# A hybrid mLSTM and SSD decoder layer on one core: a state computed at the end, and five re-timed places

## The chip, the cores and the metric

The kernel runs on 1 core of one Trainium2 chip. The metric is device time in microseconds (us) of one execution. Engines are named as in the profile: PE (matmul) with PEld (its weight loads), DVE (vector), ACT (scalar), POOL (GpSimd) and SP, which here only issues DMAs. The engines run side by side, each takes its own instructions in order, and semaphores make one wait for another.

## The reference, cut to what matters

One layer of a decoder trunk for a prompt of 256 tokens (zero state) and a batch of 8 x 8 sample tokens (given state), 320 tokens in all, 2048 wide, all in float32.

```
u = x @ w_in                                  # 2048 -> q, k, v, o, gates, z, xbc, dt
h_m, C, n, m = mlstm_mixer(q, k, v, o, ...)   # 4 heads, 256 x 256 state each
h_s, S, ...  = ssd_mixer(z, xbc, dt, ...)     # 16 heads
x = layer_norm(ALPHA * x + concat(h_m, h_s) @ w_out, ln1_g, ln1_b)
f = (silu(g) * val) @ w_down                  # g, val = conv3(x @ w_up), width 5504 each
x = layer_norm(ALPHA * x + f, ln2_g, ln2_b)
# mLSTM state at a chunk's end:
C_new = decay * C + einsum('bsh,bshd,bshe->bhde', w_end, k, v)
n_new = decay * n + einsum('bsh,bshd->bhd', w_end, k)
```

Results are the two outputs (`y_prompt`, `y_sample`) and twelve states. `p_C` and `p_n`, the prompt's last mLSTM state, are among them; nothing else in the layer reads them. Since the prompt starts at zero, the kernel forms them at one stroke from all 256 tokens: per head, C = (w k)^T [v, 1], with the column of ones giving n.

## The kernel before, in words

Activations lie transposed: 128 features on the partitions, 320 tokens along the free axis. Each weight tile of 512 KB (`raw`) is fetched by SP, split by ACT into `hi` and by DVE into `lo` (lines 74 and 75, four 128 x 128 blocks at a time), and each block takes three fast matmuls of 320 columns at line 232: hi times the activation's high half, hi times its low half, lo times its high half. The halves are `XH`, `XL` (input), `MH`, `ML` (mixer's output) and `HH`, `HL` (FFN). `run_groups` walks over the output units, 16 k-tiles each, in steps of 4 k-tiles (12 matmuls). Splits are made four steps ahead, from at most four `raw` tiles.

Everything else is a background task, a generator in `Tasks`. While the program is written out, `tasks.clk` adds up a nominal time of the matmuls; a task that yields n goes on when the clock has moved n further (a bare `yield` is 2500), and `pump` lets tasks run after each step. So a pause in a task sets only where its instructions stand in the engines' order, between which weight matmuls. `ensure` and `drain` go on without matmuls between. On chip nothing is paused; an instruction waits for its data or its turn.

The stages, in order:

1. Start. `ones` is set and 9 matmuls on it run (the name is `warm`). `x_load` fetches the prompt in four column pieces, `xs_load` the sample as two halves of its columns (k-tiles 0 to 7 on partitions 0 to 63, 8 to 15 on 64 to 127). `x_transpose` turns each k-tile (two matmuls with the identity for the prompt; one for the sample, which for k below 8 gives k and k + 8). ACT and DVE split it into `XH`, `XL`.
2. Gates. `keep_x` adds XH and XL on POOL, multiplies with the gate weights `gw` (8 + 16 columns of w_in, fetched by SP as many short runs at lines 466 and 467), in four portions c, and stores x to DRAM (`xT`). The SSD tasks wait for the gates.
3. Mixer, beside the matmuls of w_in. SSD tasks, then for each of 4 mLSTM heads: `ml_scores`, `ml_chunks` (the sample's states, in sets n0 = 0, 2, ..., 14), `ml_out` (the head's output and its group norm, with `rsqrt` as three rounds on DVE), `o_task`, `mix_parts`. `ml_prompt_state` transposes k, scales it (`kt`), multiplies it with `VT` (v by tokens, with the column of ones), copies the result out and stores `p_C`.
4. w_out, whose first four units need the four parts of the mixer's output in turn (`ensure(("mix", s))`); first norm; the FFN in three portions (w_up, then w_down each).
5. End. `down_task` of the last portion transposes each of 16 tiles back and takes statistics (line 1571). After the last tile: aggregate all 16 (line 1644), inverse root by ACT and five DVE steps (1645 to 1652), rows of mean and bias by three matmuls on the identity (`nbr`), twelve matmuls that spread them, eight DVE steps for the prompt (line 1676), and for the sample ACT twice (1671, 1673) and POOL once (1674) per 512 columns.

Of the kernel before, what the change touches and what calls it, by code (L numbers as in the profile page):

```python
# [170 lines left out]
def _hybrid_step(ctx, tc, I, O):  # L171
# [11 lines left out]
    def f32(ap):  # L183
        return ap.bitcast(F32)
# [215 lines left out]
    def x_transpose(c, kks=range(4)):  # L400
        t = box["x", c]
        if kks[-1] == 3:
            flags.add(("xt", c))
            del box["x", c]
        for kk in kks:
            k = 4 * c + kk
            ps = bank()
            for i in range(2):
                transpose(ps[:, 128 * i:128 * i + 128], t[:, i, 128 * kk:128 * kk + 128])
            parts = [(k, 0, 256)]  # L410
            if k < 8:
                transpose(ps[:, 256:384], xs_in[:, 128 * k:128 * k + 128])
                parts = [(k, 0, NT), (k + 8, NT, 384)]
            parts = [(kx, slice(256 if a else 0, 256 if b == 256 else NT), ps[:, a:b]) for kx, a, b in parts]
            for kx, o, src in parts:
                A.activation(XH(kx)[:, o], src, AF.Copy)
            for kx, o, src in parts:
                V.tensor_tensor(XL(kx)[:, o], src, f32(XH(kx))[:, o], ALU.subtract)  # L418
# [22 lines left out]
    xs_src = I["x_sample"].rearrange("b t f -> (b t) f")  # L441

    def xs_load(eng, a, b):
        for e in range(2):
            eng.dma_start(xs_in[64 * e:64 * e + 64, a:b], xs_src[:, 1024 * e + a:1024 * e + b])
# [640 lines left out]
    def ml_prompt_state():  # L1086
        yield from wait("setup")
        pn = sm([128, 8])
        for h in range(4):
            yield from wait(("k", 2 * h + 1))  # L1090
            K = box["K"]
            ps = bank()
            for i in range(2):
                for e in range(2):
                    c = 256 * i + 128 * e
                    transpose(ps[:, c:c + 128], K[:, 2 * h + e, 128 * i:128 * i + 128])
            kt = mt("T2", [128, 2, 256])
            for i in range(2):
                A.activation(kt[:, i, :], ps[:, 256 * i:256 * i + 256], AF.Copy, scale=TT2[:, i, h:h + 1])
            yield  # L1100
            yield from wait(("v", 2 * h + 1))
            yield
            cn = mt("T2", [128, 2, 256])
            for e in range(2):
                ps = bank()
                for i in range(2):
                    mm(ps[:, 0:258], kt[:, i, 128 * e:128 * e + 128], box["VT"][:, i, h, :], i == 0, i == 1)
                A.activation(cn[:, e, :], ps[:, 0:256], AF.Copy)
                V.tensor_copy(pn[:, 2 * h + e:2 * h + e + 1], ps[:, 256:257])
                yield  # L1110
            dma(O["p_C"][0, 0, h].rearrange("(e p) f -> p e f", p=128), cn)
        ps = bank()
        transpose(ps[0:8, 0:128], pn)
        po = sm([8, 128])
        V.tensor_copy(po, ps[0:8, 0:128])
        yield
        gdma(O["p_n"][0, 0].rearrange("h (e p) -> (h e) p", p=128), po)
# [48 lines left out]
    def ml_chunks():  # L1166
# [27 lines left out]
        for h in range(4):  # L1194
# [7 lines left out]
            for x in range(2):  # L1202
# [27 lines left out]
                yield 5000  # L1230
            flags.add(("acc", h))

    def ml_out(h):
# [32 lines left out]
        rs = yield from rsqrt(mp, var, GN_EPS, [128, 3], 1500)  # L1266
# [7 lines left out]
        yield 8000  # L1274
# [261 lines left out]
    lnst = fsm([128, 3, 16, 6])  # L1536
# [16 lines left out]
    def down_task(j, m, ps):  # L1553
# [16 lines left out]
        for i in range(3):  # L1570
            V.bn_stats(lnst[:, i, m, :], pt[:, 128 * i:128 * i + 128])
        if m == 14:
            A.activation(fin["sd"], fin["eps"], AF.Sqrt)
# [6 lines left out]
    def times_g(m, pt):  # L1580
# [4 lines left out]
        V.tensor_tensor(r2[:, c], pt[64:128, 256:384], gbc[64:128, c], ALU.mult)  # L1585

    def gb_rows():
# [22 lines left out]
    for j in range(3):  # L1610
# [13 lines left out]
        if j == 2:  # L1624
# [15 lines left out]
    mv, var, nb2, rs, u = fsm([128, 3, 2]), fsm([128, 3]), fsm([128, 3]), fsm([128, 3]), fsm([128, 3])  # L1640
    nbc, nbr = fsm([128, 3, 5], F32R), fr("dg", [5, 384], F32R)
    G.memset(f32(nbc), 1.0)
    for i in range(3):
        V.bn_aggr(mv[:, i, :], lnst[:, i, :, :])
    A.activation(fin["sd"], mv[:, :, 1], AF.Sqrt, bias=fin["eps"][:, 0:1])
    V.tensor_scalar(var, mv[:, :, 1], LN_EPS, None, ALU.add)
    V.reciprocal(rs, fin["sd"])
    V.tensor_tensor(u, rs, rs, ALU.mult)
    V.tensor_tensor(u, u, var, ALU.mult)
    V.tensor_scalar(var, u, 0.375, -1.25, ALU.mult, ALU.add)  # L1650
    V.tensor_tensor(u, u, var, ALU.mult)
    V.scalar_tensor_tensor(rs, u, 1.875, rs, ALU.add, ALU.mult)
    V.scalar_tensor_tensor(nb2, mv[:, :, 0], -1.0, rs, ALU.mult, ALU.mult)
    V.tensor_copy(nbc[:, :, 0:2], bcl(nb2, 2))
    V.tensor_tensor(nbc[:, :, 2], nb2, f32(nbc[:, :, 0]), ALU.subtract)
    ps = bank()
    for i in range(3):
        transpose(ps[0:5, 128 * i:128 * i + 128], f32(nbc[:, i, :]))
    for i in range(3):
        t = slice(128 * i, 128 * i + 128)  # L1660
        V.tensor_copy(nbr[:, t], ps[0:5, t])
    times_g(15, fin["pt"])
    ys = O["y_sample"].rearrange("b t f -> (b t) f")
    for c in range(4):
        s = slice(512 * c, 512 * c + 512)
        for i in range(3):
# [3 lines left out]
            if i == 2:  # L1670
                A.activation(t, t, AF.Copy, scale=rs[64:128, i:i + 1])
                w2 = fr("rx", [128, 512])[64:128]
                A.activation(w2, w[64:128, :], AF.Copy)
                G.tensor_tensor(t, t, w2, ALU.add)  # L1674
            else:
                V.scalar_tensor_tensor(t, t, rs[:, i:i + 1], w, ALU.mult, ALU.add)
# [4 lines left out]
    dma(*late)
# [64 lines left out]
```

## Time and profile before

| | us |
|---|---|
| median of 3 runs | 1546.82 |
| lowest, highest | 1544.77, 1548.61 |
| the profiled execution | 1550.87 |
| its span, first to last instruction | 1549.0 |
| PE busy within it | 1521.4 |
| DVE, ACT, POOL busy | 980.7, 773.4, 306.1 |

PE is busy nearly all the time, so what counts is where it isn't, where its granted clock is low, and how much it is given to do. A page of the profile has the whole; the other views cut it by stretches of time, by waiting engine, or row by row. A row of the timeline gives the start, the length, the engine and line, then output <- inputs; a float32 matmul stands there as two instructions, a fast one (`fp32r` operands) as one. Rows of PE overlap, since a matmul is listed up to its end in the pipeline: the distance from start to start is what one costs.

### The profile page before, as it was taken

How to read it: one execution, taken by the hardware profiler on the slowest of the kernel's cores; microseconds unless marked ns; L12 is line 12 of the kernel's file. 1: busy time of each engine (PE TensorE's matmuls, PEld its weight loads, DVE VectorE, ACT ScalarE, POOL GpSimd, SP SyncE). 2: the span in 40 equal slices, each digit the busy share in tenths (PEclk: the TensorE clock that was granted, in tenths of full speed). 3: DMA queues.
4: the chain of work that ended last, by engine and by line, in shares of the span. 5: the costliest groups of instructions: out<-in, count | busy, mean ns of one | idle time of the engine just before them, and what ended most of it. 6: DMA issues, size and time to landing. Idle time of an engine off the chain costs nothing.

```text
span 1549.0 us, 28113 instructions
## 1 busy us (share of the span) xinstructions
PE 1521.4 (98%) x10518; PEld 1488.8 (96%) x10518; DVE 980.7 (63%) x1959; ACT 773.4 (50%) x1540; POOL 306.1 (20%) x651
## 2 busy tenths in 40 slices
PE   8999999999999999999999999999999999999996
PEld 7999999998999999999999999999999999999995
DVE  4676557666687587687777445566544555656765
ACT  3655434444545454566665345555433555555332
POOL 5213331134411142233330000000000000002201
PEclk8999999999999999999999999999999999999997
DMA  9556677577665554455544454554454555455542
GB/s 252 161 150 163 183 208 225 160 211 226 209 204 174 193 180 138 126 165 149 150 150 140 154 147 146 163 150 138 149 157 146 148 151 163 141 149 170 159 145 77
DMA packets 268900, 254.39 MB, mean 164 GB/s; under 512 B 18513, under 2 KB 263265, under 8 KB 268636
## 3 DMA queue, kind: packets, MB, share of 16 engines
q1 hardware_dynamic: 263612, 248.49, 53.8%
q0 software_dynamic: 4848, 3.91, 1.0%
q8 instruction: 82, 1.34, 0.4%
q14 instruction: 54, 0.44, 0.1%
q10 hardware_dynamic: 304, 0.20, 0.0%
HBM read 231.56 MB, written 20.43 MB: 163 GB/s over the span
## 4 chain that ended last, share of the span: by engine, by line
PE 93%; DVE 2%; DMA 2%; POOL 1%; ACT 1%; issue 1%; SPq 1%; POOLq 0%; DVEq 0%; ACTq 0%
PE bk L232 90%; PE bk L238 2%; DMA T<-w_in 1%; DVE lo L75 1%; DMA rx<-xT 0%; SPq L61 0%; ACT hi L74 0%; POOL big L1674 0%; SPq L466 0%; ACT MH L1320 0%; POOL T L193 0%; POOL T L968 0%; POOL T L811 0%; DVE HL L1531 0%; POOL T L981 0%
## 5 line engine op out<-in xcount | busy, mean ns | idle before, releaser
L75 DVE TENSOR_TENSOR lo<-raw,hi 128x512 fp32r<-128x512 f32 (+2 forms) x800 | 558.0, 708 | 393.5 <-ACT hi L74 390.6
L74 ACT ACTIVATE hi<-raw 128x512 fp32r<-128x512 f32 (+2 forms) x800 | 486.3, 616 | 454.3 <-PE bk L232 429.5
L232 PE MATMUL bk<-big,hi 128*128 128x320 f32 (+1 forms) x2752 | 609.5, 310 | 0.0
L232 PEld LDWEIGHTS bk<-big,hi 128*128 128x128 f32 x2752 | 462.1, 188 | 0.0
L232 PE MATMUL bk<-big,lo 128*128 128x320 f32 (+1 forms) x1376 | 426.6, 310 | 0.4 <-DVE lo L75 0.4
L232 PE MATMUL bk<-XH,hi 128*128 128x320 f32 x832 | 269.0, 323 | 0.8 <-ACT hi L74 0.8
L232 PEld LDWEIGHTS bk<-big,lo 128*128 128x128 f32 x1376 | 259.3, 188 | 0.7 <-DVE lo L75 0.7
L232 PE MATMUL bk<-XL,hi 128*128 128x320 f32 x832 | 258.9, 311 | 0.0
L232 PE MATMUL bk<-XH,lo 128*128 128x320 f32 x832 | 258.8, 311 | 0.0
L232 PE MATMUL bk<-HH,hi 128*128 128x320 f32 x688 | 214.2, 311 | 0.0
L232 PE MATMUL bk<-HH,lo 128*128 128x320 f32 x688 | 212.6, 309 | 0.0
L232 PE MATMUL bk<-HL,hi 128*128 128x320 f32 x688 | 212.5, 309 | 0.0
L232 PEld LDWEIGHTS bk<-XH,hi 128*128 128x128 f32 x832 | 158.1, 190 | 12.0 <-issue 7.9
L232 PEld LDWEIGHTS bk<-XL,hi 128*128 128x128 f32 x832 | 158.1, 190 | 0.9 <-DVE XL L418 0.4
L232 PEld LDWEIGHTS bk<-XH,lo 128*128 128x128 f32 x832 | 157.7, 190 | 0.2 <-DVE lo L75 0.2
L193 POOL TENSOR_SCALAR fst<-c 128x18 f32<-128x18 f32 x86 | 22.5, 269 | 566.9 <-ACT c L1508 566.7
L1515 DVE SCALAR_TENSOR_TENSOR c<-c,fcol,c 128x336 f32<-128x336 f32 x172 | 97.3, 567 | 58.4 <-ACT c L1513 55.3
L232 PEld LDWEIGHTS bk<-HL,hi 128*128 128x128 f32 x688 | 129.2, 188 | 0.0
L232 PEld LDWEIGHTS bk<-HH,hi 128*128 128x128 f32 x688 | 129.2, 188 | 0.0
L232 PEld LDWEIGHTS bk<-HH,lo 128*128 128x128 f32 x688 | 129.1, 188 | 0.0
L232 PE MATMUL bk<-MH,lo 128*128 128x320 f32 x256 | 80.1, 313 | 2.4 <-DVE lo L75 2.4
L232 PE MATMUL bk<-MH,hi 128*128 128x320 f32 x256 | 80.3, 314 | 0.3 <-ACT hi L74 0.3
(330 smaller groups left out, 1470.3 us busy)
## 6 DMA issues: line engine op xcount, KB each, us to landing
raw<-ffn_w_up SPq DMA_DIRECT2D x172, 512.0 KB, 3.9
raw<-w_in SPq DMA_DIRECT2D x100, 512.0 KB, 4.2
raw<-ffn_w_down SPq DMA_DIRECT2D x71, 512.0 KB, 3.5
raw<-w_out SPq DMA_DIRECT2D x32, 512.0 KB, 5.1
T<-state_mlstm_C SPq DMA_DIRECT2D x32, 256.0 KB, 5.5
s_C<-T SPq DMA_DIRECT2D x32, 256.0 KB, 4.0
T<-state_ssm SPq DMA_DIRECT2D x8, 512.0 KB, 6.9
s_ssm<-T SPq DMA_DIRECT2D x8, 512.0 KB, 6.7
```

The source lines that it names most:

```text
L74: nc.scalar.activation(h, src, AF.Copy)
L75: nc.vector.tensor_tensor(l, src, h.bitcast(F32), ALU.subtract)
L193: G.tensor_scalar(out, in_, 1.0, 0.0, ALU.mult, ALU.add)
L232: nc.tensor.matmul(out, lhsT=lhsT, rhs=rhs, start=start, stop=stop)
L238: nc.tensor.transpose(out, in_, ident[b:b + p, b:b + p])
L1515: V.scalar_tensor_tensor(c[:, 0:336], xp[:, j:j + 336], fcol[:, j, i:i + 1], c[:, 0:336], ALU.mult, ALU.add)
```

## The change

Five edits at once.

- `ml_prompt_state` keeps the transposes and `kt`, and stores `kt` and the two prompt rows of `VT` to DRAM (`d_kt`, `d_vt`: per head 256 KB and 258 KB, eight DMAs on SP). The 16 float32 matmuls, their copies and the stores of `p_C` move to the very end: `p_operands` fetches the operands back during the last w_down (two DMAs of 512 KB, eight of 129 KB, on SP), and `p_state(h)` computes heads 0 to 2 ahead of the second norm's last transposes, head 3 between the first and the second 512 columns. `p_n` is written from there.
- The start: 13 matmuls on `ones` in place of 9 and four more between; `x_sample` laid out so that one transpose gives the k-tiles k and k + 1 (512-byte runs in place of 1024 and longer ones); the first weight split stands between the first and the second k-tile; k-tiles 0 and 1, then 2 and 3 together.
- `keep_x`: the first pause 11500 in place of 8000.
- Head 3: no pauses within `rsqrt` or after the last set of `ml_chunks`, 3000 in place of 8000 ahead of the transposes.
- The second norm: tiles 0 to 14 aggregated early (while the last tile is still being multiplied), the inverse root by one POOL instruction (`pow`), `nbr` copied in one instruction, the sample first in each 512 columns, and the sample's stores issued by ACT in place of SP.

```
-    for _ in range(9):
+    for _ in range(13):
         mm(warm[:, 0:128], ones, ones, True, True)
...
-            yield 1000 if c else 8000
+            yield 1000 if c else 11500
...
+            dma(d_kt[:, :, h, :], kt)
+            yield from wait(("v", 2 * h), ("v", 2 * h + 1))
             yield
-            cn = mt("T2", [128, 2, 256])
-            for e in range(2):
-                ps = bank()
-                for i in range(2):
-                    mm(ps[:, 0:258], kt[:, i, 128 * e:128 * e + 128], box["VT"][:, i, h, :], i == 0, i == 1)
...
+            dma(d_vt[:, :, h, :], box["VT"][:, 0:2, h, :])
...
-                yield 5000
+                yield 5000 if n0 < 14 else 0
...
-        rs = yield from rsqrt(mp, var, GN_EPS, [128, 3], 1500)
+        rs = yield from rsqrt(mp, var, GN_EPS, [128, 3], 1500 if h < 3 else 0)
...
-        yield 8000
+        yield 8000 if h < 3 else 3000
...
             x_transpose(0, [0])
+            st.split_to(0)
+            x_transpose(0, [1])
+            for _ in range(4):
+                mm(warm[:, 0:128], ones, ones, True, True)
...
+            for i in range(3):
+                V.bn_aggr(amv[:, i, :], lnst[:, i, :, :])
+            V.tensor_copy(agg[:, :, 1], amv[:, :, 0])
+            V.tensor_scalar(agg[:, :, 2], amv[:, :, 1], 1920.0, 2048.0 * LN_EPS, ALU.mult, ALU.add)
...
+    def p_state(h):
+        for e in range(2):
+            ps = bank()
+            for i in range(2):
+                mm(ps[:, 0:258], fin["k"][i][:, h, 128 * e:128 * e + 128], fin["v"][i, h], i == 0, i == 1)
+            t = fr("c", [128, 258])
+            A.activation(t, ps[:, 0:258], AF.Copy)
+            dma(O["p_C"][0, 0, h, 128 * e:128 * e + 128, :], t[:, 0:256])
+            pcopy(pn[:, 2 * h + e:2 * h + e + 1], t[:, 256:257])
...
+    G.tensor_tensor(rs, mv[:, :, 1], nhalf, ALU.pow)
...
+    for h in range(3):
+        p_state(h)
...
+        if c == 1:
+            p_state(3)
...
-        for i in range(3):
+        for i in (2, 0, 1):
...
+                if c:
+                    nc.scalar.dma_start(*late)
```

How it moves instructions. At the start, on PE, before (`T_3` is the prompt's piece, `T_2` the sample, `hi_173` and `lo_174` the first split):

```order
L232 MATMUL bk_79<-ones 128x128 x9
L238 MATMUL bk_161<-ident,T_3_90 128x128 x2
L238 MATMUL bk_161<-ident,T_2_89 128x128
L238 MATMUL bk_177<-ident,T_3_90 128x128 x2
L238 MATMUL bk_177<-ident,T_2_89 128x128
L232 MATMUL bk_157<-XH_165,hi_173 128x320
L232 MATMUL bk_157<-XL_169,hi_173 128x320
L232 MATMUL bk_157<-XH_165,lo_174 128x320
```

And now, the same place on PE:

```order
L232 MATMUL bk_81<-ones 128x128 x13
L238 MATMUL bk_167<-ident,T_3_96 128x128 x2
L238 MATMUL bk_167<-ident,T_2_95 128x128
L238 MATMUL bk_179<-ident,T_3_96 128x128 x2
L232 MATMUL bk_81<-ones 128x128 x4
L232 MATMUL bk_163<-XH_171,hi_175 128x320
L232 MATMUL bk_163<-XL_173,hi_175 128x320
L232 MATMUL bk_163<-XH_171,lo_176 128x320
```

One sample transpose went, and matmuls on `ones` now stand on both sides of the transposes. Further on, the first gate matmuls stand behind 132 weight matmuls, where 96 stood ahead of them before.

Head 3's group norm on DVE, before (`rsu`, `rsy` are the rounds of the inverse root, `lo` a weight split, line 1321 the split of the mixer's output):

```order
L301 SCALAR_TENSOR_TENSOR rsy_5972<-rsu_5973,rsy_5972 128x3
L75 TENSOR_TENSOR lo_5981<-raw_5789,hi_5980 128x512
L1285 COPY T_560_5998<-bk_5808 128x320
L1321 TENSOR_TENSOR ML_6004<-T_134_1566,MH_6002 128x640 x2
L299 TENSOR_TENSOR rsu_5973<-rsy_5972 128x3
L300 SCALAR_TENSOR_TENSOR rsu_5973<-rsu_5973,sm_5965 128x3
L301 SCALAR_TENSOR_TENSOR rsy_5972<-rsu_5973,rsy_5972 128x3
L75 TENSOR_TENSOR lo_6018<-raw_5829,hi_6017 128x512
```

And now, on DVE (lines 1257 and 1258 end the group norm's arithmetic):

```order
L301 SCALAR_TENSOR_TENSOR rsy_5952<-rsu_5953,rsy_5952 128x3
L299 TENSOR_TENSOR rsu_5953<-rsy_5952 128x3
L300 SCALAR_TENSOR_TENSOR rsu_5953<-rsu_5953,sm_5945 128x3
L301 SCALAR_TENSOR_TENSOR rsy_5952<-rsu_5953,rsy_5952 128x3
L1257 TENSOR_TENSOR sm_5943<-sm_5942,rsy_5952 128x3
L1258 SCALAR_TENSOR_TENSOR sm_5944<-sm_5935,sm_5943 128x3
L75 TENSOR_TENSOR lo_5973<-raw_5753,hi_5972 128x512
L75 TENSOR_TENSOR lo_5989<-raw_5753,hi_5988 128x512
```

The norm is one block of 25 DVE instructions, and two weight splits in a row stand behind it. On PE, head 3's last product (`num`, third slice) stands 84 weight matmuls ahead of its transposes, where it was 144, and 48 behind the last set's first matmuls, where it was 108.

The end on PE, before (`bk_17989`: the last tile's transposes; `fsm_18001`: mean rows; `rows`, `dg`: the spreading):

```order
L238 MATMUL bk_17989<-ident,big_6320 128x128 x3
L238 MATMUL bk_18018<-ident,fsm_18001 5x128 x3
L232 MATMUL bk_18027<-rows_16775,dg_18002 128x512
L232 MATMUL bk_18031<-rows_16775,dg_18002 128x512
L232 MATMUL bk_18035<-rows_16775,dg_18002 128x512
L232 MATMUL bk_18041<-rows_16775,dg_18002 128x512
```

And now on PE, from the second half of head 2 on (`c` and `rx` hold the fetched operands):

```order
L232 MATMUL bk_18036<-c_17496,rx_17210 128x258
L232 MATMUL bk_18036<-c_17498,rx_17282 128x258
L238 MATMUL bk_18043<-ident,fsm_17988 5x128 x3
L232 MATMUL bk_18050<-rows_16739,dg_17989 128x512
L232 MATMUL bk_18055<-rows_16739,dg_17989 128x512
L232 MATMUL bk_18059<-rows_16739,dg_17989 128x512
L232 MATMUL bk_18063<-c_17584,rx_17210 128x258
L232 MATMUL bk_18063<-c_17586,rx_17282 128x258
```

The twelve products of heads 0 to 2 stand between the last tile's transposes and the mean rows, and head 3's four behind the first three spreading matmuls.

More of the change, by code (lines that the diff above doesn't have):

```diff
@@ L383, in _hybrid_step @@
     xT = dp.tile([128, 16, NT], F32, name="xT")
+    d_kt, d_vt = dp.tile([128, 2, 4, 256], F32, name="d_kt"), dp.tile([128, 2, 4, 258], F32, name="d_vt")
     box = {}
@@ L409, in x_transpose @@
                 transpose(ps[:, 128 * i:128 * i + 128], t[:, i, 128 * kk:128 * kk + 128])
[L410 to L418, printed above, removed]
+            if k % 2 == 0:
+                transpose(ps[:, 256:384], xs_in[:, 64 * k:64 * k + 128])
+                parts = [(slice(0, NT), ps[:, 0:NT])]
+                box["xs"] = ps
+            else:
+                parts = [(slice(0, 256), ps[:, 0:256]), (slice(256, NT), box.pop("xs")[:, NT:384])]
+            for o, src in parts:
+                A.activation(XH(k)[:, o], src, AF.Copy)
+            for o, src in parts:
+                V.tensor_tensor(XL(k)[:, o], src, f32(XH(k))[:, o], ALU.subtract)
     def keep_x():
@@ L1100, in ml_prompt_state @@
             yield
-            yield from wait(("v", 2 * h + 1))
+            dma(d_kt[:, :, h, :], kt)
+            yield from wait(("v", 2 * h), ("v", 2 * h + 1))
             yield
-            cn = mt("T2", [128, 2, 256])
-            for e in range(2):
-                ps = bank()
-                for i in range(2):
-                    mm(ps[:, 0:258], kt[:, i, 128 * e:128 * e + 128], box["VT"][:, i, h, :], i == 0, i == 1)
[L1108 to L1117, printed above, removed]
+            dma(d_vt[:, :, h, :], box["VT"][:, 0:2, h, :])
+            yield
     def ml_ops():
@@ L1312, in each_x @@
     def each_x(u, s, kk):
-        if u == s == 0 and kk < 3:
-            x_transpose(0, [kk + 1])
+        if u == s == 0 and kk == 1:
+            x_transpose(0, [2, 3])
     MH, ML = Halves("MH"), Halves("ML")
@@ L1535, in _hybrid_step @@
     fin = {}
-    lnst = fsm([128, 3, 16, 6])
+    lnst, agg, amv = fsm([128, 3, 15, 6]), fsm([128, 3, 9]), fsm([128, 3, 2])
     def fstate():
@@ L1585, in times_g, with p_operands @@
         V.tensor_tensor(r2[:, c], pt[64:128, 256:384], gbc[64:128, c], ALU.mult)
+    def p_operands():
+        yield from wait(("h", 42), "gb")
+        yield 10000
+        fin["k"], fin["v"] = [], {}
+        for i in range(2):
+            t = fr("rx", [128, 4, 256])
+            dma(t, d_kt[:, i, :, :])
+            fin["k"].append(t)
+            yield 5000
+        for h in range(4):
+            for i in range(2):
+                fin["v"][i, h] = fr("c", [128, 258])
+                dma(fin["v"][i, h], d_vt[:, i, h, :])
+            yield 5000
+    def p_state(h):
+        for e in range(2):
+            ps = bank()
+            for i in range(2):
+                mm(ps[:, 0:258], fin["k"][i][:, h, 128 * e:128 * e + 128], fin["v"][i, h], i == 0, i == 1)
[3 more added lines that the diff above has]
+            pcopy(pn[:, 2 * h + e:2 * h + e + 1], t[:, 256:257])
     def gb_rows():
@@ L1606, in gb_rows @@
         fin["rows"] = rows
+        flags.add("gb")
     tasks.add(ln1(), front=True)
@@ L1636, in _hybrid_step @@
     tasks.drain()
-    mv, var, nb2, rs, u = fsm([128, 3, 2]), fsm([128, 3]), fsm([128, 3]), fsm([128, 3]), fsm([128, 3])
+    mv, nb2, rs, nhalf = fsm([128, 3, 2]), fsm([128, 3]), fsm([128, 3]), fsm([128, 3])
     nbc, nbr = fsm([128, 3, 5], F32R), fr("dg", [5, 384], F32R)
+    pn, w2s = fsm([128, 8]), fr("rows", [128, 2048])
+    G.memset(nhalf, -0.5)
     G.memset(f32(nbc), 1.0)
     for i in range(3):
[L1644 to L1652, printed above, removed]
+        V.bn_aggr(mv[:, i, :], agg[:, i, :])
+    G.tensor_tensor(rs, mv[:, :, 1], nhalf, ALU.pow)
     V.scalar_tensor_tensor(nb2, mv[:, :, 0], -1.0, rs, ALU.mult, ALU.mult)
@@ L1665, in _hybrid_step @@
         s = slice(512 * c, 512 * c + 512)
-        for i in range(3):
+        if c == 1:
+            p_state(3)
+        if c == 2:
+            pt = bank()
+            transpose(pt[0:8, 0:128], pn)
+            po = fsm([8, 128])
+            A.activation(po, pt[0:8, 0:128], AF.Copy)
+            gdma(O["p_n"][0, 0].rearrange("h (e p) -> (h e) p", p=128), po)
+        for i in (2, 0, 1):
             t = fin["r2"][:, s] if i == 2 else fin["r01"][:, i, s]
```

29 lines of the change are left out of this document (12 added, 17 removed).

## The prediction

> **What bounds it now.** I read the page's busy times first, then the waits of PE, then busy time and clock by stretches, then the rows at each place that the change touches.
>
> ```profile
> PE 1521.4 (98%) x10518; PEld 1488.8 (96%) x10518; DVE 980.7 (63%) x1959; ACT 773.4 (50%) x1540; POOL 306.1 (20%) x651
> ```
>
> PE is idle for 27.6 us of the span. The view of waits on PE (total, times, longest) says where:
>
> ```profile
> PE bk L238 <- DVE fsm L1655: 4.5, 1, 4.5
> PE bk L232 <- DMA T<-w_in: 3.3, 1, 3.3
> ...
> PE bk L232 <- DVE T L1080: 2.4, 2, 1.3
> ```
>
> The second norm's mean rows at the end (4.5), the gate weights (3.3), two waits in the mixer. By stretches (length, then busy us and count of PE, PEld, DVE, ACT, POOL; PE clock; DMA share; GB/s):
>
> ```profile
> 7.20:14.20 7.00, 6.13 (x22) 4.99 (x23) 3.71 (x11) 4.00 (x12) 4.24 (x8) 0.53 1.10 306
> ...
> 32.30:38.20 5.90, 5.90 (x26) 4.88 (x27) 0.69 (x1) 0.63 (x1) 0.00 (x0) 0.50 0.81 259
> ...
> 375.00:380.00 5.00, 3.87 (x31) 3.33 (x30) 2.99 (x6) 3.37 (x7) 3.66 (x8) 1.00 0.12 12
> ...
> 414.80:417.20 2.40, 1.11 (x11) 0.66 (x9) 1.54 (x3) 2.39 (x6) 1.47 (x3) 1.00 0.01 3
> 417.10:421.00 3.90, 3.90 (x13) 3.33 (x13) 3.85 (x8) 1.76 (x4) 3.71 (x7) 0.56 0.32 59
> 491.80:494.60 2.80, 0.79 (x5) 0.37 (x3) 2.70 (x7) 1.97 (x4) 0.92 (x1) 1.00 0.01 3
> 494.50:500.00 5.50, 5.47 (x27) 5.47 (x28) 3.75 (x10) 3.13 (x6) 0.00 (x0) 0.69 0.50 149
> ...
> 1531.00:1536.50 5.50, 1.08 (x4) 0.54 (x5) 3.92 (x19) 1.01 (x2) 0.00 (x0) 0.71 0.00 0
> 1536.50:1549.00 12.50, 5.20 (x12) 3.46 (x11) 6.04 (x11) 4.20 (x7) 5.04 (x4) 0.50 0.64 210
> ```
>
> A wait costs twice: once as idle time, and again as a stretch at a lower clock that PE calls busy. Elsewhere PE is full, so work taken from it between 40 and 1530 us shortens the run one for one, if no other engine becomes late.
>
> **Part 1, the start.**
>
> ```profile
> 7.30 0.84 PE L238 MATMUL bk<-ident,T 128*128 128x128 f32 x4 [2.31 <-DMA T<-x_sample]
> 8.88 0.69 DVE L75 TENSOR_TENSOR lo<-T,hi 128x512 fp32r<-128x512 f32 x1
> 8.90 0.63 PE L232 MATMUL bk<-XH,hi 128*128 128x320 f32 x1 [0.76 <-ACT hi L74]
> 9.49 0.62 DVE L418 TENSOR_TENSOR XL<-bk,XH 128x320 fp32r<-128x320 f32 x2
> ...
> 14.21 0.41 PE L232 MATMUL bk<-XH,hi 128*128 128x320 f32 x1
> ...
> 14.75 0.31 PE L232 MATMUL bk<-XH,hi 128*128 128x320 f32 x1
> ...
> 17.68 0.31 PE L232 MATMUL bk<-XH,lo 128*128 128x320 f32 x1
> ```
>
> The first twelve weight matmuls take from 8.90 to 14.21, most at half clock (0.53). From 14.75 to 17.68 there are 20 steps: 0.147 each at full clock. The sample still lands at 7.3, since the same 16 DMA engines carry the same bytes (the 512-byte runs could make it a few tenths later), so the first weight matmul stays near 8.7. What changes is the clock: PE works from 1.0 to 6.8 on `ones` and prompt transposes, and in this trace it regains full clock about 5 us after work resumes (8.90 to some 14; and up to 38.2 in the stretch from 32.3). Then DVE paces the four k-tiles: from 8.0, one split of 0.69 and four pairs of 0.62, with gaps until 11.5; the thirteenth matmul at 11.8. That is **-2.4**. With the old clock for the twelve it would be -0.9; the end on the other side is -2.9.
>
> **Part 2, the gate weights.**
>
> ```profile
> 28.66 0.31 PE L232 MATMUL bk<-XH,lo 128*128 128x320 f32 x1
> ...
> 32.27 1.30 PE L232 MATMUL bk<-T,T 128*32 128x320 f32 x8 [3.30 <-DMA T<-w_in]
> ```
>
> PE stood from 28.97 to 32.27 and then ran 5.9 us at clock 0.50, half of it lost: 3.3 + 2.9 = 6.2. Now 36 more weight matmuls stand ahead (36 x 0.147 = 5.3): PE comes at 28.97 - 2.4 + 5.3 = 31.9, less two transposes. The same queue on SP brings the gate weights at 32.2, so 0.6 stays: **-5.6** (-4.2 if they land 1.4 later). The weights for the 36 are of `raw` tiles that SP issued ahead of the gate weights.
>
> [...]
>
> **Part 3, the prompt's state out of the mixer.** Removed there: 16 float32 products, 32 instructions on PE, one transpose, 8 copies each on ACT and DVE, 4 DMAs. A run of eight:
>
> ```profile
> 340.19 2.01 PE L232 MATMUL bk<-T,T 128*128 128x258 f32 x8
> 341.85 0.50 PE L232 MATMUL bk<-XH,hi 128*128 128x320 f32 x1
> ```
>
> From 340.19 to 341.85 is 1.66, with the slower first step behind them 1.85. Four times that is 6.6 to 7.4; I take **-7.0**. Added: eight stores on SP, 2.1 MB for 1 MB of `p_C`. Weight loads queue behind them on SP, and each waits for one copy that was issued a pause earlier. A tile's time to landing is the last number of the page's row:
>
> ```profile
> raw<-w_in SPq DMA_DIRECT2D x100, 512.0 KB, 4.2
> ```
>
> Up to four `raw` tiles, 96 matmuls or 14 us, lie ahead, so the stores cost 0. The ten fetches among the weight loads of the last w_down wait for buffers that are long free, under the same 14 us: 0. If SP did block, PE would pay (rival D).
>
> **Part 4, head 3.** At 414.8 PE lost 1.3 idle and 3.9 x 0.44 = 1.7 of clock, waiting for a PSUM bank that the scores held (line 1080). The same pattern at 375 cost 1.1. The order now puts two steps of weight matmuls between scores and products for head 3, where one stood; head 2 keeps one. So the last of the two should go: **-2.0** (0 to -3.0; not all, since DVE is as busy there). At 491.8 PE lost 2.0 idle and 5.5 x 0.31 = 1.7, waiting for `lo` behind DVE's group norm and mixer splits. What stands there now:
>
> ```profile
> 480.67 3.57 DVE L75 TENSOR_TENSOR lo<-raw,hi 128x512 fp32r<-128x512 f32 x2 [0.40 <-ACT hi L74]
> ...
> 484.57 0.41 DVE L1258 BATCH_NORM_STATS2 sm<-T 128x6 f32<-128x256 f32 x1
> ...
> 488.14 0.16 DVE L301 SCALAR_TENSOR_TENSOR rsy<-rsu,rsy 128x3 f32<-128x3 f32 x1
> ```
>
> The block's first 17 instructions took 484.57 to 488.30, 3.7 us; 8 more at 0.2 make 5.3. Ahead of it stand two copies and a mixer split, so the next `lo` comes about 12.5 us after head 3's last product, and PE, with four steps of splits in hand and six transposes between, wants it after 11.8. A wait near 1 us, with some clock, is left of 3.7: **-2.0** (+1.0 to -3.7). The transposes themselves come 84 weight matmuls (12 us) behind the product and the block ends within that.
>
> The last product waits for the gather of the sample's part:
>
> ```profile
> 460.80 1.08 PE L232 MATMUL bk<-T,T 128*32 128x257 f32 x16
> ...
> 462.71 2.00 POOL L811 DMA_DIRECT2D T<-T  x4 [10.49 <-ACT T L1210]
> ...
> DMA to landing us min/median/max: 1.6/3.0/5.7
> ```
>
> 460.80 to 464.71, then 3.0: 6.9 us, up to 9.6. PE now has 48 x 0.147 and 1.5 us of products between, 8.5, where it had over 16: **+0.5** (0 to +2.0).
>
> **Part 5, the end.**
>
> ```profile
> 1530.57 0.69 DVE L1571 BATCH_NORM_STATS2 fsm<-bk 128x6 f32<-128x128 f32 x3 [0.53 <-PE bk L238]
> ...
> 1535.88 0.68 DVE L1661 CAST dg<-bk 5x128 fp32r<-5x128 f32 x3 [0.98 <-PE bk L238]
> ...
> 1537.90 0.59 ACT L1673 ACTIVATE rx<-bk 64x512 f32<-64x512 f32 x1 [2.92 <-PE bk L232]
> 1538.39 0.70 ACT L1671 ACTIVATE big<-big,fsm 64x512 f32<-64x512 f32 x1
> 1538.63 5.10 POOL L1674 TENSOR_TENSOR big<-big,rx 64x512 f32<-64x512 f32 x4 [91.45 <-DVE big L1676]
> ...
> 1544.69 0.55 SPq L1681 DMA_DIRECT2D y_sample<-big  x1
> ```
>
> Before, `nbr` was ready at 1536.56, POOL's four additions ended at 1543.73, the last store was issued by 1545.24. Now, on the same clock, the early aggregation delays the last tile's addition by 0.2, and PE runs 24 float32 instructions from 1530.75, 24 x 0.215 = 5.2, to 1535.9. Beside them run the statistics, the three short aggregations, POOL's `pow` and three DVE steps. Short aggregations and evictions have these rows (group's mean in ns; a like eviction; two DMA issues on ACT's queue):
>
> ```profile
> L1259 DVE BATCH_NORM_AGGREGATE sm<-sm 128x2 f32<-128x6 f32 x12 | 2.2, 182 | 0.4
> ...
> 418.32 0.39 ACT L1242 ACTIVATE T<-bk 128x258 f32<-128x258 f32 x1 [0.75 <-PE bk L232]
> ...
> 1.20 1.18 ACTq L445 DMA_DIRECT2D T<-x_sample  x2
> ```
>
> 0.7 + 0.55 + 0.65 end at 1532.7 plus `pow`, which no row shows; up to 3.2 us of it is hidden under PE. Mean rows 0.5, `nbr` 0.6: 1537.0, 0.4 later than before, and the first three spreading matmuls end by 1537.7. Head 3's eight instructions take to 1539.5. From there ACT carries the chain to the third piece: two evictions' rest 0.6, scale 0.7, copy 0.6, DMA issue 0.6, `p_n` 0.2, scale and copy 1.3, issue 0.6, scale and copy 1.3, gaps 0.3: 1545.7. POOL's last addition 1.3 and the store's issue 0.6: 1547.6, against 1545.24. **+2.2** (+1 with a shorter `pow` path and no issue delay; +5 if `pow` takes over 3 us and POOL's small copies queue).
>
> **Sum.** -2.4 - 5.6 - 7.0 - 2.0 - 2.0 + 0.5 + 2.2 = -16.3. The profiled span of 1549.0 becomes 1532.7; that execution's own time, 1550.87, becomes 1534.6. It lay 4.05 above the median of the runs shown (and above all three), so against the median 1546.82 I expect 1530.5, and say **1531**. All smallest together: -0.9 - 4.2 - 6.6 + 0 + 1.0 + 2.0 + 5 = -3.7, 1543; all largest: -2.9 - 6.2 - 7.4 - 3.0 - 3.7 + 0 + 1 = -22.2, 1524.6.
>
> **Rivals.**
> A, the end gives back half: `pow` or POOL's eight small copies come late and ACT's queue, now with stores, stretches; +10 instead of +2.2. For it: POOL was the pace at the end already (5.10 in four). Against: 3.2 us of cover. 1538.3.
> B, the last heads crowd: with DVE's and POOL's steps closer, PE waits as long as before and longer, so part 4's -4.0 and half of part 3 are lost and 3 us of new waits come: 1541. For it: two splits took 3.57 where two take 1.4 elsewhere, while POOL worked at 480 to 484. [...]
> C, the gate weights land later too (SP's issue follows the same full DMA engines), and the wait stays: -5.6 lost, 1536.1.
> D, slower: SP, in order, is held by a store or fetch that waits, and weights come late. With 4.2 to landing under a cover of 14, a hold reaches PE only from some 9 us on; to end 4.6 above 1546.8 eight such holds would have to cost PE 2.6 each: 1552. Against: the four `p_C` stores stood in the same queue, and PE never waited for a `raw` tile.
>
> **Chances.** The forecast (1525 to 1536) 0.70, A 0.10, B 0.08, C 0.07, D 0.05. Range for 8 in 10: 1525 to 1540. About 0.3% (4.6 us) is what a measurement can tell from no change. Faster by more: the forecast, A, C and most of B: 0.92; within: 0.04; slower: 0.04.
>
> **What would show it.** Full clock by about 9 us and the thirteenth weight matmul near 12; no wait over 1 us for the gate weights; at most one wait on the scores' eviction; under 2 us lost where w_out begins; no 258-column products between 320 and 430 us but 32 instructions past the last tile; the last store issued 1 to 4 us later, counted from the last weight matmul. Wrong would be: PE waiting for `raw` in the mixer or the last w_down, or an end over 5 us longer.

## The result, and the profile after

The changed kernel took 1538.4 us (median of 4 runs, 1537.34 to 1541.38) against 1547.71 for the kernel before: a ratio of 0.994, 95% interval 0.9924 to 0.9956. That is 9.3 us less, where 15.8 was forecast; the range of 1525 to 1540 holds it, but the band of 1525 to 1536 that had 0.70 does not. Its profiled execution took 1537.98 (span 1536.2), 12.8 us of span less than the one shown of before, where the sum said 16.3.

The page's first line, and PE's waits (total, times, longest):

```profile
PE 1515.6 (99%) x10534; PEld 1483.4 (97%) x10534; DVE 979.2 (64%) x1946; ACT 773.3 (50%) x1539; POOL 313.5 (20%) x661
PE bk L232 <- DVE lo L75: 2.8, 4, 1.5
PE bk L238 <- ACT T L1261: 2.4, 1, 2.4
PE bk L232 <- DVE T L1082: 2.3, 2, 1.5
```

The two longest waits of before, the mean rows (4.5) and the gate weights (3.3), are gone. The waits in the mixer are not: the scores' PSUM bank (now line 1082) still costs 2.3 in two waits, `lo` 1.5 at one place, and there is a new wait of 2.4 on ACT's last group-norm step (line 1261).

The best way to see where time went is to compare the start of the same weight matmul, counted from the first, in both traces. Up to the gates and some way past them, from the timeline of after (the 13th, the 97th, the gate matmuls, the 217th):

```profile
11.78 0.31 PE L232 MATMUL bk<-XH,hi 128*128 128x320 f32 x1
26.69 0.31 PE L232 MATMUL bk<-XH,hi 128*128 128x320 f32 x1
33.33 0.75 PE L232 MATMUL bk<-T,T 128*32 128x320 f32 x8
49.77 0.31 PE L232 MATMUL bk<-XH,hi 128*128 128x320 f32 x1
```

and the 217th in before:

```profile
57.04 0.31 PE L232 MATMUL bk<-XH,hi 128*128 128x320 f32 x1
```

The 13th starts at 11.78 (before: 14.21), the gate matmuls run without a wait, and behind them PE is 57.04 - 49.77 = 7.3 us ahead. It is still 7.3 ahead at the 1725th, before the mLSTM heads' products, 14.1 at the 2757th, inside w_out, and 14.2 at the last. So the stretch of the heads and w_out's beginning brought 6.8.

Head 2 and the beginning of w_out in the timeline of after:

```profile
376.00 0.94 DVE L1074 SCALAR_TENSOR_TENSOR T<-T,TT,T 128x256 f32<-128x256 f32 x3 [2.20 <-DMA T<-d_m]
377.02 1.28 ACT L1076 ACT_TABLE_LOAD   x1 [4.82 <-DVE T L1074]
379.56 0.23 DVE L1082 TENSOR_TENSOR T<-bk,T 64x64 f32<-64x64 f32 x1
379.94 0.47 PE L232 MATMUL bk<-T 32*128 32x256 f32 x5 [1.54 <-DVE T L1082]
...
480.62 0.42 PE L232 MATMUL bk<-MH,lo 128*128 128x320 f32 x1 [1.53 <-DVE lo L75]
...
482.01 0.74 ACT L1314 ACTIVATE MH<-T 128x640 fp32r<-128x640 f32 x1 [5.65 <-DVE T L1284]
...
483.17 1.57 ACT L1261 ACTIVATE T<-T,sm,sm 128x256 f32<-128x256 f32 x3
484.79 0.87 PE L238 MATMUL bk<-ident,T 128*128 128x128 f32 x6 [2.44 <-ACT T L1261]
```

and by stretches:

```profile
7.00:14.00 7.00, 6.51 (x41) 5.37 (x41) 4.59 (x11) 4.65 (x12) 4.53 (x9) 1.00 1.11 301
...
380.00:384.70 4.70, 4.70 (x22) 4.38 (x23) 4.57 (x11) 1.34 (x3) 0.00 (x0) 0.64 0.67 206
484.00:488.00 4.00, 3.21 (x24) 3.21 (x25) 2.30 (x5) 3.18 (x7) 0.00 (x0) 1.00 0.24 76
```

At head 2, DVE waits 2.20 for the mask's row `d_m`; exponent, table load and product follow late, the scores' bank comes free late, PE waits 1.54 and then runs 4.7 us at a clock of 0.64. None of this stood in before, whose wait there was 1.1 with full clock behind it. Where w_out begins, PE loses 1.53 + 2.44 of idle time, at full clock; before it lost 2.0 and 1.7 of clock.

The end, with the last weight matmul of each kernel, before:

```profile
1529.13 0.31 PE L232 MATMUL bk<-HH,lo 128*128 128x320 f32 x1
```

and after:

```profile
1514.92 0.31 PE L232 MATMUL bk<-HH,lo 128*128 128x320 f32 x1
...
1516.15 5.39 PE L232 MATMUL bk<-c,rx 128*128 128x258 f32 x24
...
1517.43 0.89 POOL L1672 TENSOR_TENSOR fsm<-fsm,fsm 128x3 f32<-128x3 f32 x1 [84.46 <-DVE fsm L1671]
...
1518.76 0.17 DVE L1675 TENSOR_TENSOR fsm<-fsm,fsm 128x3 fp32r<-128x3 f32 x1
...
1521.90 0.55 DVE L1682 CAST dg<-bk 5x384 fp32r<-5x384 f32 x1 [2.34 <-PE bk L238]
...
1531.89 0.47 ACTq L1709 DMA_DIRECT2D y_sample<-big  x1
```

`pow` takes 0.89, the norm's values are there at 1518.93, and PE's 24 instructions cover that until 1521.4. The last store is issued by 1532.36, 17.4 after the start of the last weight matmul, where it was 16.1 before: +1.3.

### The profile page after: what moved, and what is told of

It reads as the page before. It is cut to its first block, busy times and chain, and to the rows that moved or that the text cites. A ratio compares the mean times of both kernels' runs of the same rounds, so it can differ in the third digit from the quotient of the medians.

```text
span 1536.2 us, 28188 instructions
## 1 busy us (share of the span) xinstructions
PE 1515.6 (99%) x10534; PEld 1483.4 (97%) x10534; DVE 979.2 (64%) x1946; ACT 773.3 (50%) x1539; POOL 313.5 (20%) x661
## 4 chain that ended last, share of the span: by engine, by line
PE 94%; DVE 2%; DMA 1%; ACT 1%; issue 1%; SPq 0%; POOL 0%; ACTq 0%; POOLq 0%; DVEq 0%
PE bk L232 92%; PE bk L238 2%; DMA T<-d_m 1%; DVE lo L75 0%; DMA T<-x_sample 0%; DMA raw<-w_in 0%; ACT hi L74 0%; POOL big L1702 0%; DVE T L1212 0%; ACT XH L418 0%; SPq L1172 0%; DVE XL L420 0%; DVE HL L1525 0%; DVE rx L1627 0%; ACT T L1261 0%
## 5 line engine op out<-in xcount | busy, mean ns | idle before, releaser
L232 PE MATMUL bk<-XH,hi 128*128 128x320 f32 x832 | 265.8, 319 | 0.1
```

The source lines that it names most:

```text
L232: nc.tensor.matmul(out, lhsT=lhsT, rhs=rhs, start=start, stop=stop)
```

## The experiments

All times are medians; each kernel ran beside the kernel before, whose median was 1548.3, 1548.1 and 1547.9 in the three sets. Kernels of different sets are compared by their medians; many of their 95% intervals overlap, and then only the traces can tell. Two theories ran through the experiments. N: each part gave its gain where it stands, and what is missing was lost at new waits in the last heads. R: the profiled run of before had lost more to the clock than a common run, so the sum counted what the median never lost.

**Start and gate alone, put into the kernel before.**

```
-    for _ in range(9):
+    for _ in range(13):
...
-            yield 1000 if c else 8000
+            yield 1000 if c else 11500
...
+            st.split_to(0)
+            x_transpose(0, [1])
```

> The kernel before with parts 1 and 2 alone (the start, and the gates 36 weight matmuls later). In the two profiles the first 200 weight matmuls are 7.3 us earlier after the change (2.3 by the 36th, 4.9 more behind the gates). Theory N (the parts gave their gain where they stand, and what is missing was lost at new waits in the last heads): 7 us under the kernel before, some 1540.5. Rival R (the profiled run of before was a slow one, 3 us above its median, because of its cold stretches at the start and the gate, so that the median never held that loss): 3 to 4 us under the kernel before, some 1544.

1542.7 (ratio 0.9961, 0.9949 to 0.9973): 5.6 us, between the two.

**The kernel before, profiled again.** No edit.

> The kernel before once more, profiled. Theory R (the profiled run shown of before had more cold stretches than its common runs, mean clock 0.988 against 0.990 to 0.994, so that the sum counted clock that the median never lost): a mean clock of 0.990 or more, a time of 1546 to 1549, and less than 5.9 us lost to the clock in the first 60 us or less than 3.3 us in the mixer's last heads. Rival: the same stretches at the same clock; then the difference lies elsewhere.

1548.33, clock 0.992. By stretches, the first of them the start, the second the gate weights, the third the scores of head 3:

```profile
7.20:14.20 7.00, 5.68 (x26) 4.62 (x25) 4.01 (x11) 4.30 (x13) 4.25 (x8) 0.76 1.10 297
30.00:36.00 6.00, 4.33 (x24) 3.84 (x25) 0.31 (x1) 0.63 (x1) 0.00 (x0) 0.76 0.97 263
415.20:420.20 5.00, 4.91 (x30) 4.28 (x31) 4.92 (x9) 2.41 (x7) 4.74 (x8) 1.00 0.36 86
```

Beside it the same place of head 3 in the first profile of before:

```profile
416.50:421.50 5.00, 4.94 (x22) 4.22 (x23) 4.92 (x10) 2.36 (x6) 4.74 (x8) 0.66 0.35 80
```

Same program, same wait (1.30 and 1.29), and one time full clock, the other time 0.66. Adding busy time x (1 - clock) over slices of 2 us, the second profile lost 3.2 in the first 60 us and 1.7 in the last heads; the first lost 5.9 and 3.3. That is 4.3 less, but not all of it is time, since in the first k-tiles the clock alone doesn't set the pace (at 1.00 the changed kernel takes 8.35 to 11.78 for its first twelve weight matmuls, 3.4 where 12 x 0.147 make 1.8): the second execution is 2.5 shorter, 1.8 of it by the 217th weight matmul (55.28) and 2.1 by the 2757th (528.46). R holds with this size: some 2.5 us of what I set out to remove was this one execution's. The run with start and gate alone fits it: its 217th weight matmul (49.38) is 5.9 ahead of this second profile, and the medians differ by 5.6.

**The old first pause before the gates.**

```
-            yield 1000 if c else 11500
+            yield 1000 if c else 8000
```

> The changed kernel with the first pause ahead of the gates as it was, 8000. The forecast's part 2 (3.3 us of wait for the gate weights and 2.9 us of half clock behind it): 5 to 6 us slower than the changed kernel, some 1544. Theory R (the profiled run of before lost more to the clock than a common one; profiled again, it lost 1.7 us in the stretch behind the gates): 4 to 4.5 us slower, some 1542.5. Rival C of the forecast (the weights land later with the earlier start, so the wait is there either way): no difference.

1541.75 (0.9965, 0.9952 to 0.9979), 3.4 above the changed kernel. The wait is back:

```profile
32.75 0.75 PE L232 MATMUL bk<-T,T 128*32 128x320 f32 x8 [3.62 <-DMA T<-w_in]
```

Past the gates this profile is 56.91 - 49.77 = 7.1 behind the changed kernel's, but its span is only 3.8 longer: its order in the mixer is another one, with 0.9 of wait where w_out begins in place of 1.53 and 2.44. Rival C is out; in these profiles half of what the gates lose came back elsewhere.

**The old start.** The edits of the start taken out of the changed kernel.

```
-    for _ in range(13):
+    for _ in range(9):
...
-            st.split_to(0)
-            x_transpose(0, [1])
...
-        if u == s == 0 and kk == 1:
-            x_transpose(0, [2, 3])
+        if u == s == 0 and kk < 3:
+            x_transpose(0, [kk + 1])
```

> The changed kernel with the old start (9 matmuls on ones, the sample in two halves, the first split behind the first k-tile's transposes). The forecast's part 1: 2.4 us slower than the changed kernel, 1540.8. Theory R (the common run of before loses 1.5 us to the clock there and not 2.8): 1 to 1.5 us slower, 1539.7. Rival (the start's gain is given back at the gate weights, which land at their own time): no difference.

1540.7, but from 1538.3 to 1544.1 (0.9958, 0.9944 to 0.9972). The trace speaks for the rival. The 97th and the 217th weight matmul with the old start:

```profile
28.24 0.31 PE L232 MATMUL bk<-XH,hi 128*128 128x320 f32 x1
49.48 0.31 PE L232 MATMUL bk<-XH,hi 128*128 128x320 f32 x1
```

At the 97th the new start is 1.55 ahead, at the 217th 0.29 behind. Between them lies the third piece of the prompt. In the changed kernel:

```profile
24.10 3.14 DVE L75 TENSOR_TENSOR lo<-raw,hi 128x512 fp32r<-128x512 f32 x3 [3.12 <-ACT hi L74]
27.16 2.10 DVE L420 TENSOR_TENSOR XL<-bk,XH 128x320 fp32r<-128x320 f32 x6
27.70 0.42 PE L232 MATMUL bk<-XL,hi 128*128 128x320 f32 x1 [0.70 <-DVE XL L420]
```

and with the old start:

```profile
27.25 1.41 DVE L419 TENSOR_TENSOR XL<-bk,XH 128x256 fp32r<-128x256 f32 x4
```

The new layout spreads the sample over all four pieces, so pieces three and four carry six `XL` steps in place of four, and DVE reaches them behind three weight splits at the same time as before (27.2). PE, which came earlier, waits 0.70 for the third piece and 0.84 for the fourth (0.50 with the old start). The other profiles with the new start agree: where the gates come late too, their 217th lies between 49.38 and 50.99, and the old start's 49.48 is among the earliest. The 2.3 between the medians need then not be the start's own: the profile with the old start has 3.35 lost to the clock in the last heads, the changed kernel's 1.7. What the start is worth stays open, between 0 and 2 us.

**The prompt's state in the mixer again.**

```
-            dma(d_kt[:, :, h, :], kt)
-            yield from wait(("v", 2 * h), ("v", 2 * h + 1))
+            yield from wait(("v", 2 * h + 1))
...
+                    mm(ps[:, 0:258], kt[:, i, 128 * e:128 * e + 128], box["VT"][:, i, h, :], i == 0, i == 1)
...
-    for h in range(3):
-        p_state(h)
```

> The changed kernel with the prompt's state computed in the mixer again and the new end without it. Theory N (16 float32 products and one transpose cost PE 7 us in the mixer and, at the end, lie for a good part beside the second norm): the mixer 6 to 7 us longer, the end 4 to 5 us shorter than in the changed kernel, so 2 us slower than it, some 1540.5. Rival C (the mixer is paced by DVE and ACT, so products taken from PE come back as waits): the mixer 3 us longer, the end as much shorter, so 1 to 2 us faster than the changed kernel, some 1537.

1544.7 (0.9983, 0.9974 to 0.9993), 6.3 above the changed kernel: the largest effect of all. In the profiles the stretch of the heads is 8.5 longer, with idle time and clock loss together much as in the changed kernel (9.7 against 9.2), so nearly all of it is PE's work; the 32 instructions make 6.9 of it at 0.217 each. From the last weight matmul to the end of the span the kernel is only 2.6 shorter, not 4 to 5. Its end:

```profile
1527.87 0.49 PE L238 MATMUL bk<-ident,fsm 128*5 128x128 f32 x3 [2.76 <-DVE fsm L1686]
...
1531.04 6.51 SPq L1709 DMA_DIRECT2D y_prompt<-big  x8
```

PE stands for 2.76 where the products lay, its clock is 0.50 from 1529.0 on (the twelve spreading matmuls take 5.48), and the last of eight stores on SP is issued by 1537.55, later than any other. Rival C of this run, that work taken from PE returns as waits, is out.

**Head 3's old pauses.**

```
-                yield 5000 if n0 < 14 else 0
+                yield 5000
...
-        rs = yield from rsqrt(mp, var, GN_EPS, [128, 3], 1500 if h < 3 else 0)
+        rs = yield from rsqrt(mp, var, GN_EPS, [128, 3], 1500)
...
-        yield 8000 if h < 3 else 3000
+        yield 8000
```

> The changed kernel with the three pauses of head 3 as they were before. Theory N (the shorter pauses took one wait at the scores away and brought as much back as waits of 1.5 and 2.4 us where w_out begins): within 1.5 us of the changed kernel, some 1538.5, with no wait of PE for the group norm's ACT steps (2.4 before w_out's third part) but one at head 3's scores. Rival (the forecast's part 4, that the shorter pauses are worth 4 us): 4 us slower than the changed kernel, some 1542.

1537.7 (0.9937, 0.9924 to 0.995), 0.7 under the changed kernel. The longest of PE's waits from 320 to 530:

```profile
PE bk L232 <- DVE T L1082: 2.3, 2, 1.1
PE bk L232 <- issue: 1.7, 1, 1.7
PE bk L232 <- ACT MH L1314: 1.2, 1, 1.2
```

The 2.4 on the group norm is gone, 1.2 on the last mixer split came, and the two at the scores are there, 1.1 each. No gain of the shorter pauses shows, and the rival's 1542 (a ratio of 0.996) lies outside the interval.

**`d_m` fetched early.**

```
+        Mb = sm([128, NT])
+        dma(Mb, d_m[0:1].broadcast_to([128, NT]))
...
-            Mb = mt("T2", [128, NT])
-            dma(Mb, d_m[h:h + 1].broadcast_to([128, NT]))
...
+            if h < 3:
+                dma(Mb, d_m[h + 1:h + 2].broadcast_to([128, NT]))
```

> The changed kernel with the row d_m of the mask fetched into a buffer of its own right behind the scores of the head before, in place of 4000 units ahead of its use behind other DMAs of SP. Theory N (DVE waited 2.2 us for d_m at head 2, so the scores' PSUM bank came free late, PE stood 1.5 us and then ran 3.5 us of busy time at half clock): the waits on d_m go, PE's wait at head 2 falls under 1 us and the cold stretch behind it goes; 2 to 3 us under the changed kernel, some 1536. Rival (the bank is late since DVE and ACT are full there, exponent and table load, whatever d_m does): same as the changed kernel, 1538.4, with the wait still there.

1535.7 (0.9927, 0.9914 to 0.9939), 2.7 under the changed kernel. PE's waits from 320 to 530:

```profile
PE bk L238 <- ACT T L1263: 2.4, 1, 2.4
PE bk L232 <- DVE lo L75: 2.2, 2, 1.5
PE bk L232 <- ACT T L1234: 0.5, 1, 0.5
PE bk L232 <- DVE T L1082: 0.4, 1, 0.4
```

At head 2 the mask starts 2.3 earlier (counted from the 1725th weight matmul), PE's wait is gone and the clock stays at 1.00 there and through the heads. N holds by the trace; the time alone would not show it, since the intervals overlap and two of the five runs took 1539.

**The operands' stores on ACT.**

```
-            dma(d_kt[:, :, h, :], kt)
+            nc.scalar.dma_start(d_kt[:, :, h, :], kt)
...
-            dma(d_vt[:, :, h, :], box["VT"][:, 0:2, h, :])
+            nc.scalar.dma_start(d_vt[:, :, h, :], box["VT"][:, 0:2, h, :])
```

> The changed kernel with the eight stores of the operands issued by ACT in place of SP. Theory O (d_m is late for head 2 since 12 weight matmuls and four chunk products lie between its issue and the mask where 36 and eight transposes lay): the wait of DVE on d_m and PE's wait at head 2 stay, same time as the changed kernel, 1538.4, or 1 us more, since ACT pays 0.55 for each issue. Rival S (the stores on SP hold d_m up): the wait on d_m goes, 2 to 3 us faster, some 1536.

1539.8 (0.9953, 0.9938 to 0.9969), and the wait at head 2 stays:

```profile
380.36 0.47 PE L232 MATMUL bk<-T 32*128 32x256 f32 x5 [1.93 <-DVE T L1082]
```

So SP's new stores are not the reason. What the change moved is the order: the pause of 4000 nominal units between `d_m`'s issue and the mask of head 2 holds 36 weight matmuls in the program of before, and 24 in the changed one (not 12, as I had counted), since other work is counted into it. Moving the state does this: with the old pause at the gates it is 24 as well, and DVE waits 4.1 for `d_m` there (5.5 in two waits), while with the state in the mixer it is 36 and DVE does not wait there. That run waits 1.7 at head 3, as the one with start and gate alone does; there the pause holds 24 weight matmuls as before, so that wait came with the start and the later gates, and its cause is open.

**The end with two and two heads** (with the early `d_m`).

```
-    for h in range(3):
+    for h in range(2):
         p_state(h)
...
-        if c == 1:
-            p_state(3)
...
+        if c % 2:
+            p_state(2 + c // 2)
```

> The kernel with the early d_m, and at the end the products of heads 0 and 1 alone ahead of the mean rows, head 2's behind the second 512 columns and head 3's behind the last; p_n stored by SP. Theory N (the mean rows wait for 24 products, 1516.1 to 1521.4, though their values are there at 1518.9; the sample's four additions then stretch over 8 us, since ACT evicts head 3 between them): mean rows at 1519.6 on that clock, four additions in 6 to 7 us, end 1.5 to 2 us shorter, 1534. Rival (the end is set by all of ACT's and SP's work there, in whatever order): same as the kernel with the early d_m, 1535.7.

1537.4 (0.9932, 0.992 to 0.9944), 1.7 over the early `d_m` alone. By stretches at its end:

```profile
1519.00:1522.00 3.00, 2.42 (x10) 1.77 (x11) 2.17 (x4) 2.44 (x5) 1.34 (x2) 1.00 0.27 92
1522.00:1529.50 7.50, 7.50 (x19) 5.07 (x18) 3.80 (x6) 3.56 (x7) 4.43 (x7) 0.54 1.00 320
```

The mean rows did come earlier, but PE then had a gap of 0.6, its clock fell to half for 7 us, and head 3's eight instructions took 3.4 where they took 2.0. The gain expected is not there. That the gap brought the fall is not shown: the next kernel has the same gap of 0.64 at this place, and its clock stayed at 1.00 over the 10 us behind it.

**Head 3's pauses again, with early `d_m` and the end of two and two heads:** the old pauses, then only those inside the group norm as they were.

```
-        rs = yield from rsqrt(mp, var, GN_EPS, [128, 3], 1500 if h < 3 else 0)
+        rs = yield from rsqrt(mp, var, GN_EPS, [128, 3], 1500)
```

> As the kernel with two and two heads at the end, and head 3's pauses as they were. Theory N (the shorter pauses put the group norm in one block, 25 DVE steps with the weight splits behind it, and the transposes ahead of their data: waits of 1.5 and 2.4 us that no longer pause has): 0.5 to 1.5 us faster than with the shorter pauses, 1533. Rival (the shorter pauses are worth something once d_m is early): 1 to 3 us slower, 1536.

1536.5, from 1531.8 to 1543.0 (0.9926, 0.9908 to 0.9943): too wide to tell.

> As the kernel with two and two heads at the end, with the pauses inside head 3's group norm as they were and the other two short. Theory N: the block of DVE steps is cut again, so the wait of 1.5 on the split goes, and the transposes come 36 weight matmuls (5.3 us) later, so their wait of 2.4 goes; the wait on the last mixer split of the old pauses (1.2) doesn't come: 3 us faster than with the short pauses, 1531. Rival: a wait of some 1 us stays or comes elsewhere, 1533.

1533.5, 1531.57 to 1533.61 (0.9906, 0.9891 to 0.992). PE's waits from 320 to 530, all of them:

```profile
PE bk L232 <- issue: 1.2, 1, 1.2
PE bk L232 <- DVE lo L75: 1.0, 2, 0.7
PE bk L232 <- ACT T L1234: 0.5, 1, 0.5
PE bk L232 <- DVE T L1082: 0.4, 1, 0.4
```

The 2.4 and the 1.5 at w_out's beginning are gone, and nothing took their place (a wait of 1.4 with no releaser shown stood in the kernel with the short pauses too).

**The same with the changed kernel's end.**

> The changed kernel with d_m early and the pauses inside head 3's group norm as they were, its other two pauses short, and the end as in the changed kernel. Theory N: the waits on d_m and those where w_out begins are gone as in the kernel that also had two and two heads at the end (1533.5), and the end with 24 products ahead of the mean rows is no worse than with 16, since PE then has no gap in which its clock falls: 1532 to 1533.5, 5 us under the changed kernel. Rival (two and two heads were worth 1.5 us): 1535.

1534.2, 1533.8 to 1534.6 (0.9914, 0.99 to 0.9928). Both are 4 to 5 us faster than the changed kernel and 14 faster than before; between the two the runs don't tell, so no gain of two and two heads shows.

## Why the prediction held, and fell short

The direction was right and the time lies in the range, near its upper end; 1531 was 7.4 too low, and the band that had 0.70 missed. The time is that of rival A (1538.3), but by luck: A's reason, a late end, is not what happened. Of the 7.4, 3.4 are terms of the sum and 4 the step from the profiled run to the median. In the profiles the start gave -2.35, the gates -4.9, heads and w_out together -6.9 where -10.5 was forecast, and the end +1.3 (+1.4 to the end of the span). Of the signs named, two did not come: there were still two waits on the scores' bank, and 4.0 us, not under 2, were lost where w_out begins.

- **Part 1, start, -2.4.** In place it gave that: 2.35 at the 37th weight matmul, the 13th at 11.78, clock 1.00. But the step stopped there. It did not ask what is late next, and against the old start the lead is gone by the 217th.
- **Part 2, gates, -5.6.** The wait is gone, as forecast. The two profiles give -4.9. With the old pause PE is 7.1 behind past the gates, but the median is only 3.4 longer, since the heads come out otherwise. The half clock behind the wait (2.9 of the 5.6) was this profile's; profiled again, it cost 1.7.
- **Part 3, state, -7.0.** Right in mechanism and a little small: 8.5 in the stretch of the heads by the run with the state put back, 6.3 net of the end. No wait of PE shows for the stores and fetches, as said, and rival D is out. What I had not costed is that it and the later gates move the nominal clock, and with it pauses in the heads.
- **Part 4, head 3, -4.0 and +0.5.** This is the step that failed: nothing came of it. With its own pauses undone the kernel is not slower, and of the three it was the missing pauses inside the group norm that brought the waits where w_out begins: with these alone put back, and `d_m` early, the waits are gone and the time is 3.9 us less with one end and 1.5 with the other, the last within the noise. The wait at head 3's scores did shrink (0.79 at full clock, after 1.3 and 1.7 of clock), but head 2's, which I had costed as unchanged, grew from 1.1 to 1.5 and lost 1.7 of clock. And "the transposes come 12 us behind the product and the block ends within that" left out ACT: its order puts a mixer split that waits for DVE (line 1314) ahead of the group norm's last step, so the transposes waited 2.44 (ACT began that split at 482.01, 2.0 us after DVE's block had ended). The gather cost 0 and not 0.5. Rival B had the first half of this, waits as long as before, without its reason.
- **Part 5, end, +2.2.** Measured +1.3; the row of mean values was copied by 1522.45, where the forecast, moved by the 14.6 us that the 24 products start earlier (1516.15 for 1530.75), said 1522.4. Rival A is out: `pow` took 0.89.
- **From the profile to the median.** I took 4.05 off both kernels alike. The profiled run of before had the lowest clock (0.988, against 0.990 to 0.995 in the later runs of it), and some 2.5 us of that loss was already in my sum as gains. It can't be removed a second time. Most of the rest of the 4 is the median of three runs that I started from: 1546.82, where the later sets gave 1547.7 to 1548.3.

"A wait costs twice" held at some waits only: after 1.3 (before) and 1.54 us (after, head 2) the clock fell to 0.66 and 0.64, while the same wait of 1.3 at head 3's scores was followed by 1.00 in the second profile of before (last section).

## What to carry to other kernels

- A loss of clock after a short wait can be there in one execution and not in the next (0.66 and 1.00 here, after 1.3 us): profile the kernel twice before such a loss enters a sum, and don't take the difference between a profiled run and the median off as a constant.
- Where pauses are counted in nominal work, moving work changes how much each pause holds. After such a change look for waits on small transfers: a row of the mask that landed 2 us late cost some 2.7 us here (by medians), and a buffer of its own took that back.
- Ask of an earlier start what it then runs into. And work that had to be done was cheapest where PE otherwise stood (for 2.76 us, with the state in the mixer): 32 instructions cost 8.5 us in the mixer and 2.6 at the end.

## What the runs showed of the hardware

Waits of PE of 1.3 (before), 1.54 (after) and 1.98 us (start and gate alone) were followed by a clock of 0.66, 0.64 and 0.66 over the next 5 us; waits of 1.30 (before, again), 1.93 (stores on ACT) and 1.99 us (state in the mixer) at the same places were followed by 1.00. The length of the wait didn't decide it. By busy time x (1 - clock) each of the first three cost 1.7 us.

Cut where it changes, the granted clock of the first profile of before and of the one of after reads 1.00 or 0.50, and a mean of 0.66 over 5 us is a stretch of 3.41 us at 0.50 with full clock around it. In the first profile of before half clock begins at 31.48 (for 6.83 us), 417.19 and 495.69 (3.41 each); these starts are 113 and 23 times 3.413 us apart. Head 3's scores, each profile cut at such distances from its own changes, the first of before and then the second:

```profile
413.78:417.19 3.41, 2.12 (x17) 1.56 (x16) 1.53 (x3) 3.40 (x6) 1.46 (x3) 1.00 0.01 2
417.19:420.60 3.41, 3.41 (x10) 2.85 (x10) 3.36 (x7) 1.33 (x4) 3.30 (x6) 0.50 0.25 38
...
412.04:415.46 3.42, 2.12 (x18) 1.75 (x18) 1.30 (x5) 3.08 (x5) 1.06 (x2) 1.00 0.01 2
415.46:418.87 3.41, 3.41 (x23) 2.86 (x23) 3.37 (x6) 2.13 (x5) 3.23 (x6) 1.00 0.16 28
```

PE is busy for 2.12 us of 3.41 in both, 62%, and one is followed by half clock. Other stretches of 3.41 us from 20 to 530 us, cut the same way, with PE busy for at most 67%: in the first profile of before 0.90 (26%) and 1.71 us (50%) were followed by 0.50, 2.18 (64%) and 2.27 (67%) by 1.00; in the profile of after 1.87 (55%) by 0.50, and 1.73 (51%), 2.02 (59%) and 2.14 (63%) by 1.00. In these two profiles no stretch at full clock with PE busier than that was followed by half clock there. What decided between the others is not shown. At the end of the changed kernel PE is busy for all of the 3.41 us from 1524.46, two thirds of it with matmuls on 5 partitions, and 0.50 follows. Why is not shown.

The runs of the early `d_m` lie in two groups, three at 1535.6 to 1535.7 and two at 1539.1 and 1539.2; that is about the size of two such stretches (2 x 1.7, an estimate), and the mean clock is lower in the later group (0.995 and 0.996 against 0.997 and 0.998), but which place it was, no trace of them shows.
